# A tile of ones at address 160 instead of 192 modulo 256, in a decoder block bound by TensorE

## The chip, the cores and the metric

The kernel runs on one core of a Trainium2 chip, as one program. The time is the device time of one execution in microseconds. It was run three times before the change: median 1702.03 us, 1701.56 to 1702.17. One more execution was profiled.

## What is computed

One decoder block on 256 tokens of width 2048, all in float32 (heads, masks and gains are left out here):

```python
x = x + hybrid_mixer(rms_norm(x, g_mix), w_in, w_a2, b_a, g_gla, w_pool, pool_scale, w_branch, w_out)
x = x + memory_cross_attention(rms_norm(x, g_cross), rms_norm(mem, g_mem), w_cq, w_ckv, w_co)
x = x + conv_glu_ffn(rms_norm(x, g_ffn), w_up, conv_w, conv_b, w_down)
return rms_norm(x, g_final)

def rms_norm(x, g):
    return x * rsqrt(mean(x * x, axis=-1) + EPS) * g
```

The mixer projects with w_in (2048 x 8208), runs a gated linear attention of four heads and a pooling branch, gates and joins them with w_branch, and projects with w_out. The cross-attention reads 256 memory tokens. The FFN projects up to 2 x 5632 columns, applies a causal convolution of width 3 and a gate, and projects down. Some 77 million weights are each used once for all 256 tokens.

## The kernel before, in words

**Layout.** Activations are kept transposed: features on the 128 partitions, the 256 tokens along the free dimension, 16 chunks of 128 features. A weight matrix comes in units of 2048 x 128 (16 blocks of 128 x 128); each unit yields 128 output features for all tokens.

**Two parts for each number.** To get float32 results from the faster float32r products, each number is split in a high part, rounded to float32r, and a low part, the rest. Weights are split as they arrive: a DMA brings half a unit to a `raw` tile, ScalarE casts the high part to `wh`, VectorE subtracts for the low part `wl` (both at line 110, in `Weights.make`). An activation tile holds, for each chunk, 256 columns high and 256 columns low side by side (`Act`). `products` (lines 316 to 322) runs over the blocks of a unit and issues two matmuls for each, the *pair* that the rest of this text counts: line 321 with the block of `wh` as stationary operand against all 512 columns, line 322 with the block of `wl` against the 256 high columns only. Both add up in one PSUM tile. Stages that use these pairs are, in order: w_in (56 units: keys, queries, r, gates, pool, more gates; tiles ps_k, ps_q, ps_r, ps_g, ps_p), w_branch (br), w_out (ps_wo), the keys of the memory (ps_ck), the queries (ps_cq), the output of the attention (ps_wc), the FFN (88 units ps_up and, in thirds, ps_dn and ps_dl with ps_dt). The values are made the other way round, activations stationary and weights moving, three float32r matmuls each (va at lines 395 to 397, cv at lines 713 to 715).

**Groups in plain float32.** Between the units stand small groups of matmuls on plain float32 operands, which TensorE runs as two passes each (a transpose as one). Their stationary operands are named by `lhsT`. They are: decay gates (L459 a transpose of `a_sb`, L467 with `wa`), scores of the linear attention (L524, L513, L550), its values (L562 to L564), the norm of its heads (L579), the pooling maps (L616), the transposes of the attention weights (L755), and the RMS norms. The norms use the tile `ones`, 128 x 128, in two ways: `Sum.cols` (L270) has the sums of squares as stationary operand and one column of the ones as moving operand; `Sum.rows` (L279) has the ones as stationary operand and a 128 x 256 diagonal, `diag`, moving. L579 has the ones as stationary operand against 512 columns. At the start eight products of the ones with themselves (L348, `warm`) keep TensorE at work until the first weights are there; at the end L892, L893 and L899 use the ones for the last norm. `behind` puts each such group right after a given pair in TensorE's order.

**Order.** One planner orders the instructions of all engines at build time; TensorE's order is otherwise the order of the loops. DMAs of weights are issued from SyncE's queue as the six `raw` tiles come free.

**Addresses.** Tiles of a pool lie one behind the other in each partition, rounded up to 32 bytes; pools lie in the order of their opening, `const` first. The pools `pad1` and `pad2` put 192 and 64 bytes between others. Modulo 256 this gives: `ones` 192, `ident` 192, `a_sb` 32 and 96 (its two halves), all tiles of `big` (activations, kq, kl, v, wa, wp, so and so on) 160, `wh` 96, `wl` 160, `acc` and `diag` 160, the attention weights `pr` 224.

Of the kernel before, what the change touches and what calls it, by code (L numbers as in the profile page):

```python
# [8 lines left out]
F32 = mybir.dt.float32  # L9
# [6 lines left out]
P = 128  # L16
# [126 lines left out]
def block(ctx, tc, xT, memT, vecs, masks, wa2, wpool, w_va, w_in, w_branch, w_out, w_ckv_k, w_ckv_v, w_cq, w_co, w_up, w_down, out):  # L143
    nc = tc.nc
    PS = bass.MemoryType.PSUM
    const = ctx.enter_context(tc.tile_pool(name="const", bufs=1))
# [63 lines left out]
    nc.sync.dma_start(vec[:, V_CB:], vecs[:, V_CB:])  # L210
    eps_t = const.tile([P, 1], F32, name="eps_t")
    nc.vector.memset(eps_t, EPS)
    ones = const.tile([P, P], F32, name="ones")
    ident = const.tile([P, P], F32, name="ident")
    nc.vector.memset(ones, 1.0)
    make_identity(nc, ident)
    scrap = const.tile([P, 1], F32, name="scrap")
# [760 lines left out]
```

## Time and profile before

| | us |
|---|---|
| median of three runs | 1702.03 |
| the profiled execution | 1702.15 |
| its span, first to last instruction | 1700.4 |
| TensorE weight loads busy | 1490.3 |
| VectorE busy | 1228.0 |
| ScalarE busy | 897.2 |
| GpSimd busy | 31.7 |

TensorE's matmuls are PE, its weight loads PEld, VectorE is DVE, ScalarE ACT, GpSimd POOL, SyncE SP. A matmul's duration includes the time in which the next one already runs, so durations add up to more than the time; how fast TensorE goes is read from the starts. `L321` is line 321 of the kernel. The profile's mean DMA rate is 186 GB/s.

### The profile page before, as it was taken

The page shows a single profiled execution, that of the slowest core. Times are in us where ns is not written, and L with a number is a line of the kernel's source. Part 1 is how long each engine was busy: PE and PEld are TensorE (multiplying, and loading weights), DVE is VectorE, ACT ScalarE, POOL GpSimd, SP SyncE. Part 2 cuts the span into 40 slices and gives each one's busy share as a digit, 9 for nine tenths or more (in the row PEclk, how much of TensorE's full clock was granted, in tenths as well). Part 3 has the DMA queues.
Part 4 walks back from the last instruction along what each step waited for, and adds up shares of the span by engine and source line. Part 5 has one row for each costly group of instructions (what it writes and reads, how often), then busy time and mean ns, then how long its engine had stood idle before and what let it go on. Part 6 is the DMA issues. An engine that isn't in the chain of part 4 may idle for free.

```text
span 1700.4 us, 25992 instructions
## 1 busy us (share of the span) xinstructions
PE 1689.0 (99%) x9900; PEld 1490.3 (88%) x9900; DVE 1228.0 (72%) x1904; ACT 897.2 (53%) x1376; POOL 31.7 (2%) x137
## 2 busy tenths in 40 slices
PE   9999999999999999999999999999999999999997
PEld 9988988888888888889988888888888888888887
DVE  7687658667889755447777788775677776567776
ACT  7555456445556544445555655553355554345564
POOL 2000000000001000000000000000000000000000
PEclk9999999999999999999999999999999999999999
DMA  8665556556666566655446665666665566665563
GB/s 276 193 204 166 174 161 208 182 169 196 192 218 218 184 191 188 186 186 167 152 148 191 189 190 190 187 186 187 190 190 188 186 187 188 190 191 186 170 178 112
DMA packets 90734, 316.15 MB, mean 186 GB/s; under 512 B 10208, under 2 KB 11104, under 8 KB 90608
## 3 DMA queue, kind: packets, MB, share of 16 engines
q1 hardware_dynamic: 90464, 314.43, 59.4%
q8 instruction: 77, 1.26, 0.3%
q14 instruction: 49, 0.40, 0.1%
q10 hardware_dynamic: 144, 0.05, 0.0%
HBM read 312.35 MB, written 2.10 MB: 185 GB/s over the span
## 4 chain that ended last, share of the span: by engine, by line
PE 99%; DMA 0%; DVE 0%; SPq 0%; ACT 0%; issue 0%; DVEq 0%; ACTq 0%
PE ps_up L321 19%; PE ps_up L322 10%; PE ps_dn L321 7%; PE ps_g L321 7%; PE ps_dn L322 4%; PE ps_ck L321 3%; PE ps_g L322 3%; PE ps_wc L321 3%; PE ps_wo L321 3%; PE ps_cq L321 3%; PE br L321 3%; PE cv L714 2%; PE ps_ck L322 2%; PE cv L713 2%; PE cv L715 2%; PE ps_p L321 2%
## 5 line engine op out<-in xcount | busy, mean ns | idle before, releaser
L110 DVE TENSOR_TENSOR wl<-raw,wh 128x1024 fp32r<-128x1024 f32 (+3 forms) x602 | 718.1, 1194 | 379.4 <-ACT wh L110 371.9
L110 ACT CAST wh<-raw 128x1024 fp32r<-128x1024 f32 (+3 forms) x602 | 614.6, 1023 | 712.2 <-issue 273.2
L321 PE MATMUL ps_up<-h,wh 128*128 128x512 f32 x1408 | 493.0, 395 | 0.0
L322 PE MATMUL ps_up<-h,wl 128*128 128x256 f32 x1408 | 394.8, 280 | 0.0
L321 PEld LDWEIGHTS ps_up<-h,wh 128*128 128x128 f32 x1408 | 264.7, 188 | 61.1
L322 PEld LDWEIGHTS ps_up<-h,wl 128*128 128x128 f32 x1408 | 264.3, 188 | 0.0
L321 PE MATMUL ps_dn<-ga,wh 128*128 128x512 f32 x512 | 179.3, 395 | 0.0
L321 PE MATMUL ps_g<-h,wh 128*128 128x512 f32 x512 | 178.0, 394 | 0.0
L322 PE MATMUL ps_dn<-ga,wl 128*128 128x256 f32 x512 | 143.6, 280 | 0.0
L322 PE MATMUL ps_g<-h,wl 128*128 128x256 f32 x512 | 142.1, 277 | 0.0
L321 PEld LDWEIGHTS ps_dn<-ga,wh 128*128 128x128 f32 x512 | 96.3, 188 | 22.3
L321 PEld LDWEIGHTS ps_g<-h,wh 128*128 128x128 f32 x512 | 96.2, 188 | 20.7 <-ACT wh L110 0.2
L322 PEld LDWEIGHTS ps_g<-h,wl 128*128 128x128 f32 x512 | 96.2, 188 | 0.3 <-issue 0.2
L322 PEld LDWEIGHTS ps_dn<-ga,wl 128*128 128x128 f32 x512 | 96.1, 188 | 0.0
L321 PE MATMUL ps_ck<-me,wh 128*128 128x512 f32 x256 | 89.7, 395 | 0.0
L321 PE MATMUL ps_cq<-h,wh 128*128 128x512 f32 x256 | 87.8, 390 | 0.0
L321 PE MATMUL ps_wc<-oc,wh 128*128 128x512 f32 x256 | 87.6, 390 | 0.0
L321 PE MATMUL ps_wo<-mg,wh 128*128 128x512 f32 x256 | 87.3, 389 | 0.0
L322 PE MATMUL ps_ck<-me,wl 128*128 128x256 f32 x256 | 71.7, 280 | 0.0
L322 PE MATMUL ps_cq<-h,wl 128*128 128x256 f32 x256 | 70.7, 276 | 0.0
L322 PE MATMUL ps_wc<-oc,wl 128*128 128x256 f32 x256 | 70.5, 276 | 0.0
L322 PE MATMUL ps_wo<-mg,wl 128*128 128x256 f32 x256 | 70.5, 276 | 0.0
(321 smaller groups left out, 2765.5 us busy)
## 6 DMA issues: line engine op xcount, KB each, us to landing
raw<-w_up SPq DMA_DIRECT2D x176, 512.0 KB, 3.6
raw<-w_in SPq DMA_DIRECT2D x112, 512.0 KB, 3.9
raw<-w_down SPq DMA_DIRECT2D x64, 512.0 KB, 3.6
raw<-w_branch SPq DMA_DIRECT2D x32, 512.0 KB, 4.4
raw<-w_out SPq DMA_DIRECT2D x32, 512.0 KB, 4.4
raw<-w_ckv_k SPq DMA_DIRECT2D x32, 512.0 KB, 3.7
raw<-w_ckv_v SPq DMA_DIRECT2D x32, 512.0 KB, 3.5
raw<-w_cq SPq DMA_DIRECT2D x32, 512.0 KB, 4.3
```

Of the source, the lines that this page charges most:

```text
L110: return self.nc.scalar.copy(hi, src), self.nc.vector.tensor_sub(lo, src, hi.bitcast(F32))
L321: nc.tensor.matmul(ps, lhsT=wh, rhs=act.both(c), start=f, stop=False, skip_group_check=True)
L322: pe["last"] = nc.tensor.matmul(ps[:, 0:T], lhsT=wl, rhs=act.hi(c), start=False, stop=l, skip_group_check=True)
L713: nc.tensor.matmul(acc[t], lhsT=xh, rhs=wh, start=c == 0, stop=False)
L714: nc.tensor.matmul(acc[t], lhsT=xh, rhs=wl, start=False, stop=False)
L715: nc.tensor.matmul(acc[t], lhsT=xl, rhs=wh, start=False, stop=c == NC - 1)
```

## The change

Two tiles without any use stand around the ones in the pool `const`: 56 float32 (224 bytes) in front of them, 8 float32 (32 bytes) behind. The ones so begin 224 bytes later, at 160 modulo 256 and no longer at 192; `ident` and all that lies behind it, the other pools too, begins 256 bytes later and keeps its address modulo 256. VectorE sets both new tiles to zero.

```diff
     eps_t = const.tile([P, 1], F32, name="eps_t")
     nc.vector.memset(eps_t, EPS)
+    gaps = [const.tile([P, 56], F32, name="gap0")]
     ones = const.tile([P, P], F32, name="ones")
+    gaps.append(const.tile([P, 8], F32, name="gap1"))
     ident = const.tile([P, P], F32, name="ident")
+    for gap in gaps:
+        nc.vector.memset(gap, 0.0)
     nc.vector.memset(ones, 1.0)
     make_identity(nc, ident)
```

## Rows read from the trace of the kernel before

**Rows 1.** The page: span, TensorE's busy time, the chain that ended last.
```profile
span 1700.4 us, 25992 instructions
...
PE 1689.0 (99%) x9900; PEld 1490.3 (88%) x9900; DVE 1228.0 (72%) x1904; ACT 897.2 (53%) x1376; POOL 31.7 (2%) x137
...
PE 99%; DMA 0%; DVE 0%; SPq 0%; ACT 0%; issue 0%; DVEq 0%; ACTq 0%
```
**Rows 2.** Groups by line, TensorE, 962.5 to 1629.3 us: busy us, mean ns | idle before.
```profile
L321 PE MATMUL ps_up<-h,wh 128*128 128x512 f32 x1376 | 481.9, 395 | 0.0
...
L321 PE MATMUL ps_dn<-ga,wh 128*128 128x512 f32 x512 | 179.3, 395 | 0.0
...
L321 PE MATMUL ps_dl<-ga,wh 128*128 128x512 f32 x18 | 6.3, 395 | 0.0
```
**Rows 3.** Groups by line, TensorE, 325 to 575 us.
```profile
L321 PE MATMUL ps_wo<-mg,wh 128*128 128x512 f32 x256 | 87.3, 389 | 0.0
```
**Rows 4.** Timeline of TensorE from 961.4 us: start us, us, instruction.
```profile
961.82 0.59 PE L279 MATMUL rps_wc<-diag_wc,ones 128*128 128x256 f32 x2
...
962.60 0.40 PE L321 MATMUL ps_up<-h,wh 128*128 128x512 f32 x1
...
966.10 0.40 PE L321 MATMUL ps_up<-h,wh 128*128 128x512 f32 x1
```
**Rows 5.** Timeline of TensorE from 324 us.
```profile
323.83 1.03 PE L616 MATMUL pps<-pl,wp 128*128 128x256 f32 x4
...
325.73 0.39 PE L321 MATMUL ps_p<-h,wh 128*128 128x512 f32 x1
...
328.11 0.39 PE L321 MATMUL ps_p<-h,wh 128*128 128x512 f32 x1
```
**Rows 6.** Timeline of TensorE from 785.9 us.
```profile
786.24 0.60 PE L755 MATMUL pTps<-ident,pr 128*128 128x128 f32 x4
...
787.37 0.39 PE L321 MATMUL ps_cq<-h,wh 128*128 128x512 f32 x1
```
**Rows 7.** Timeline of TensorE from 248.3 us.
```profile
248.45 1.88 PE L579 MATMUL oss<-so,ones 128*128 128x512 f32 x4
...
252.96 0.40 PE L321 MATMUL ps_g<-h,wh 128*128 128x512 f32 x1
```
**Rows 8.** Timeline of TensorE from 61.4 us.
```profile
61.77 0.38 PE L459 MATMUL aps<-ident,a_sb 128*16 128x128 f32 x2
...
63.39 0.40 PE L321 MATMUL ps_k<-h,wh 128*128 128x512 f32 x1
```
**Rows 9.** Timeline of TensorE from 1629 us.
```profile
1629.35 0.74 PE L321 MATMUL ps_dl<-ga,wh 128*128 128x512 f32 x2
...
1631.54 0.39 PE L321 MATMUL ps_dl<-ga,wh 128*128 128x512 f32 x1
```
**Rows 10.** Groups by line, TensorE: 249.8 to 322.8, 582.6 to 660.6, 660.7 to 750.6 us.
```profile
L321 PE MATMUL ps_g<-h,wh 128*128 128x512 f32 x144 | 50.8, 398 | 0.0
...
L321 PE MATMUL ps_p<-h,wh 128*128 128x512 f32 x64 | 22.4, 395 | 0.0
...
L321 PE MATMUL ps_ck<-me,wh 128*128 128x512 f32 x224 | 78.6, 396 | 0.0
...
L714 PE MATMUL cv<-wl,me 128*128 128x512 f32 x128 | 51.0, 399 | 0.0
```
**Rows 11.** Stretches: us, then busy us by engine, clock, DMA share, GB/s.
```profile
370.00:570.00 200.00, 199.99 (x1177) 176.65 (x1176) 167.31 (x258) 115.60 (x194) 11.99 (x14) 1.00 0.64 204
...
970.00:1620.00 650.00, 650.00 (x3716) 569.14 (x3716) 480.73 (x719) 334.32 (x484) 8.43 (x84) 1.00 0.61 187
```
**Rows 12.** Timeline of the start: the memsets, the warm-up, a wait of TensorE.
```profile
0.81 0.12 DVE L159 MEMSET pad<- 128x48 f32 x2 [0.81 <-PEq L971]
...
1.14 3.78 PE L348 MATMUL warm<-ones 128*128 128x128 f32 x16 [1.14 <-DVE ones L215]
...
11.27 0.39 PE L395 MATMUL va<-wh,h 128*128 128x260 f32 x1 [1.10 <-ACT wh L110]
```
**Rows 13.** One stretch, TensorE alone: us, busy us, clock, DMA share, GB/s.
```profile
13.20:16.20 3.00, 3.00 (x16) 0.50 1.05 404
```

## The prediction, made before the changed kernel was run

> **What bounds the kernel now.** I read the page first, from the span to the chain of waits [rows 1]: TensorE is busy for 1689.0 of 1700.4 us, and the chain that ends last runs on it for 99%. So time can only come from work taken off TensorE, or from the same work done there at another rate. The second is the point here, and the groups of instructions by line show it when they are asked stretch by stretch. One unit of weights is 16 pairs (12 in the last down products): L321, the high part of the weights, 512 columns, then L322, the low part, 256 columns. Between 962.5 and 1629.3 us, where TensorE never waits, one L321 has a mean of 395 ns [rows 2]; from 325 to 575 us the same form stands at 389 ns [rows 3]. These durations overlap, so the rate itself is read from starts in the timeline. Behind the group L279 at 961.82 us ten pairs go from 962.60 to 966.10: 350 ns a pair [rows 4]. Behind the group L616 at 323.83 us seven go from 325.73 to 328.11: 340 ns [rows 5]. Same shapes, and TensorE idle in neither. The kernel has **two rates, 340 and 350 ns a pair**, and each lasts for hundreds of pairs; an L321 of 0.40 us in the timeline marks the slow one, 0.39 the fast one.
>
> What sets the rate? Each slow stretch begins right behind a small group of products in plain float32, and I compared those groups by the tile that they hold as stationary operand. There are 28 places where such a group is followed by pairs. Behind 24 of them the pairs fall to 340 ns after two or three: L467, L524, L513, L550, L562 to L564 and L616, whose stationary tiles lie at 160 modulo 256 (one row group stands for these, [rows 5]); L270, stationary the sums of squares, also at 160, and the ones only moving, one column; L755, stationary at 224 [rows 6]. Behind the other four the pairs stay at 350 ns: L579 at 248.45 [rows 7], the two L279 in the keys and the one at 961.82 [rows 4], which are all the groups with the ones, at 192, as stationary operand that are followed by pairs; and L459 at 61.77, with a stationary operand of 16 columns, slow for 14 pairs until L467 [rows 8]. Length doesn't sort them: the group L755 takes 0.60 us and L279 0.59. Nor does the moving operand: L755 streams ident, at 192, and the pairs behind it are fast. What sorts 27 of the 28 is whether the stationary operand begins at 160 or 224 (32 above a multiple of 64) or at 192 (on one). Once set, a rate stays until something breaks the order of TensorE: the next float32 group, the products L713 to L715, or the odd place at 1629.35 where two L321 stand side by side, behind which the pairs are fast [rows 9].
>
> **The change part by part.**
>
> *The ones at 160.* L279 with the ones there has the addresses modulo 256 and the form of L616: stationary 128x128 at 160, moving 128x256 at 160. L616 is followed by fast pairs 4 times of 4. So I take it that the three stretches behind L579 and L279 go at 340 ns. Their pairs: 1376 + 512 + 18 = 1906 in the FFN [rows 2], 224 in the keys, 144 + 64 = 208 in gates and pool [rows 10], 2338 together. Two or three pairs are slow behind fast groups too, so 3 x 3 come off: 2329 x 10 ns = 23.3 us. The other 1864 or so (4216 by the loops, less 2338, less 14) are fast already. Bounds: nothing, if the address isn't the cause; and above, L714 behind the slow keys stands at 399 ns [rows 10], and if it and its neighbours, 384 in all, fell to the 389 of [rows 3], 3.8 us more. I take nothing for them: their operands keep their places, and the pairs behind them are fast now.
>
> *What the faster pairs ask of the others.* In the FFN 350 to 340 asks 2.9% more of the other engines. From 970 to 1620 us VectorE is busy for 480.73 of 650 us, 74%, ScalarE for 51%, and DMA moves 187 GB/s. From 370 to 570 us, at 340 ns a pair, VectorE is at 167.31 of 200, 84%, DMA at 204 GB/s, and TensorE is busy for all but 0.01 us [rows 11]. The FFN at 340 ns would need 76% and 192 GB/s, both below what is carried there. So nothing is late next, and the sum holds in full.
>
> *The products with the ones themselves.* Two of L279 take 0.59 us and four of L616, at 160, take 1.03 [rows 4, 5]: 0.22 for each one more, the same 0.37 for the last. I take no change. Behind the warm-up, all of them are some 8 us; 3%, the only difference of rates seen here, is 0.3 us either way.
>
> *The two memsets.* VectorE sets two tiles of 48 elements in 0.12 us, so 56 and 8 elements cost some 0.06 each. They may stand ahead of the ones, for which the warm-up L348 waits, so the first product may come up to 0.12 us later. TensorE then waits 1.10 us for a cast at 11.27 [rows 12], which a DMA feeds, and that takes the delay up: nothing; without that cover 0.12. What a shifted start can touch is the clock: from 13.2 to 16.2 us, behind such waits, the granted clock is 0.50, the lower of its two levels, and 16 products take 3.0 us [rows 13] that go at 0.12 each at full clock. Having that stretch or not is worth 1.1 us either way; I take none, as the runs of before lie within 0.6.
>
> *Two rules weighed.* The Trainium skill, "TensorE: Matmul & The Clock Gate", step-by-step of a matmul, says that TensorE has two independent read ports and that "loading the next tile's weights doesn't steal SBUF read bandwidth from the running matmul"; and the Trainium skill, "SBUF — State Buffer", specifications, gives lines of 16 bytes, on which 160 and 192 both begin. By these no address of the ones could change a rate, and the time would be that of rival (d). The trace agrees in part only: two rates with the same shapes and no wait [rows 2, 3] show that something beyond two free streams costs 10 ns a pair; that it is the address, no run here has shown.
>
> **Sum.** The profiled execution took 1702.15 us, 1700.4 of it the span; 1702.15 - 23.3 = 1678.8. The median shown, 1702.03, lies 0.12 below that execution, which gives **1678.7 us**.
>
> **The rivals.** (a) is the forecast: all three stretches turn fast, 1678.7. For it: 27 of 28 groups, and that fast is what the other disturbances fall to. (b) The FFN turns fast, the keys or the gates don't: 2.2 and 2.1 us are missing, 1680.8 to 1683.0. For it: L579 streams 512 columns, a form that none of the fast groups has. (c) Only keys or gates turn: 1697.7 to 1699.9. For it: the group at 961.82 is one lone product of two passes, and the fast groups of this width have eight. (d) Nothing turns, 1702.0: the rate is set by something else that goes with these groups, such as so few passes of 256 or more columns, or the same stationary tile loaded again each time. All three groups share that, so the trace can't tell it from the address. Against it: neither explains L459, nor do few passes alone, since L755 has four. (e) Slower: everything behind the tile lies 256 bytes further. If a longer period than 256 decides which rate pairs fall to, fast stretches turn slow at 10 ns a pair: with w_out and the query and output products of the attention, 768 pairs, 7.7 us more, 1709.7; with all 1864, 18.6 us, 1720.6. It decides from some 340 pairs on. Against it: the places of all other tiles to each other stay, and the fast rate outlives every border between units now.
>
> **How the numbers follow.** (a) 0.56, (b) 0.12, (c) 0.07, (d) 0.17, (e) 0.08. A measurement of this kernel tells some 0.2%, 3.4 us, from no change. Faster: (a), (b) and half of (c), 0.72; same: (d) and the other half, 0.20; slower: 0.08. The likeliest case has its own range, 1674.5 (L713 to L715 in its favour, with the 0.3 of the ones' own products) to 1681. Ended there the range would leave more than three in ten out, and at 1700 still a quarter, so it goes to 1702.6, no change with the memsets' 0.12 and the spread of the runs: 1674.5 to 1702.6.
>
> **What would show it.** Right: behind L279, then near 959 us, successive L321 start 0.34 us apart, L321 has a mean of 389 ns in ps_up and ps_dn, in ps_ck, and in the ps_g and ps_p behind L579, and the 14 pairs behind L459 stay slow. Wrong: 395 ns in ps_up as before (then the address is not it); a stretch that is fast now at 395 (e); or TensorE waiting for wl or wh in the FFN, where the cover would be too thin.

## The result, and the profile after

The kernel with the ones at 160 takes **1679.13 us** (median of four executions, 1678.34 to 1680.02); in the same runs the kernel before took 1702.10 (1701.56 to 1702.72). The ratio is 0.9865, 95% interval 0.9848 to 0.9882. The forecast was 1678.7.

The page of the profiled execution, 1678.34 us, answers to [rows 1]: the span is 23.9 us shorter, TensorE's busy time 24.4, and the chain still runs on TensorE for 98%. The amount of work is the same.

```profile
span 1676.5 us, 25994 instructions
...
PE 1664.6 (99%) x9900; PEld 1475.7 (88%) x9900; DVE 1228.2 (73%) x1906; ACT 898.8 (54%) x1376; POOL 31.9 (2%) x137
...
PE 98%; DVE 0%; ACT 0%; DMA 0%; SPq 0%; issue 0%; DVEq 0%; ACTq 0%
```

Below the new lines everything in the kernel after stands 4 lines further down: L325 and L326 are the pair that stood at L321 and L322. Groups by line, TensorE, 957.5 to 1609.5 us (busy us, mean ns | idle before). They answer to [rows 2]: 395 has become 389; for ps_dn the same view gives 389 too.

```profile
L325 PE MATMUL ps_up<-h,wh 128*128 128x512 f32 x1376 | 468.2, 389 | 0.0
```

Timeline of TensorE behind the group of the FFN, as in [rows 4] (start us, us, instruction). From 958.06 to 960.10 are six pairs: 340 ns each, where the kernel before had 350.

```profile
956.93 0.59 PE L283 MATMUL rps_wc<-diag_wc,ones 128*128 128x256 f32 x2
...
958.06 0.39 PE L325 MATMUL ps_up<-h,wh 128*128 128x512 f32 x1
...
960.10 0.39 PE L325 MATMUL ps_up<-h,wh 128*128 128x512 f32 x1
```

The same view behind the group of the gates, as in [rows 7]: six pairs from 250.24 to 252.28, 340 ns again. The four products of the group take 1.88 us, as before.

```profile
247.83 1.88 PE L583 MATMUL oss<-so,ones 128*128 128x512 f32 x4
...
250.24 0.39 PE L325 MATMUL ps_g<-h,wh 128*128 128x512 f32 x1
...
252.28 0.39 PE L325 MATMUL ps_g<-h,wh 128*128 128x512 f32 x1
```

Behind the transpose of `a_sb`, which the change leaves alone, the pairs are as slow as in [rows 8].

```profile
61.15 0.38 PE L463 MATMUL aps<-ident,a_sb 128*16 128x128 f32 x2
...
62.07 0.40 PE L325 MATMUL ps_k<-h,wh 128*128 128x512 f32 x1
...
62.42 0.40 PE L325 MATMUL ps_k<-h,wh 128*128 128x512 f32 x1
```

Groups by line, TensorE, of the stretches of [rows 10]: gates and pool 249.4 to 322, keys 579.5 to 656.5, values 655.5 to 746 us. The keys fall from 396 to 390; the middle product of the values stays at 399.

```profile
L325 PE MATMUL ps_g<-h,wh 128*128 128x512 f32 x144 | 49.4, 392 | 0.0
...
L325 PE MATMUL ps_ck<-me,wh 128*128 128x512 f32 x224 | 76.4, 390 | 0.0
...
L718 PE MATMUL cv<-wl,me 128*128 128x512 f32 x128 | 51.0, 399 | 0.0
```

The FFN as one stretch (us; busy us of PE, PEld, DVE, ACT, POOL; clock, DMA share, GB/s), against the second line of [rows 11]: VectorE at 483.19 of 635 us is 76%, DMA at 192 GB/s, TensorE never waits.

```profile
965.00:1600.00 635.00, 635.00 (x3738) 562.25 (x3737) 483.19 (x723) 338.29 (x489) 8.33 (x84) 1.00 0.62 192
```

Counted start by start over both traces, 2413 pairs of the kernel before took about 350 ns (345 to 355) and 86 of the kernel after do: 2327 x 10 ns = 23.3 us. The other 0.6 us of the two profiled executions lie at the start, where the first pair of all begins at 55.69 in place of 56.31 us (rows of the timeline, then the stretch as above). VectorE's memsets delay the first product from 1.14 to 1.22 us, but TensorE's wait of 1.10 us in [rows 12] is now 0.55, and from 13.2 to 16.2 us the granted clock is 1.00, the upper of the two levels, where [rows 13] had 0.50.

```profile
1.22 3.15 PE L352 MATMUL warm<-ones 128*128 128x128 f32 x13 [1.22 <-DVE ones L219]
...
10.86 0.39 PE L399 MATMUL va<-wh,h 128*128 128x260 f32 x1 [0.55 <-ACT wh L110]
```

```profile
13.20:16.20 3.00, 3.00 (x28) 3.00 (x26) 3.00 (x5) 3.00 (x9) 1.81 (x2) 1.00 1.05 405
```

### The profile page after: what moved, and what is told of

It is laid out like the page before. It is cut to its first block, busy times and chain, and to the rows that moved or that the text cites. A ratio compares the mean times of both kernels' runs of the same rounds, so it can differ in the third digit from the quotient of the medians.

```text
span 1676.5 us, 25994 instructions
## 1 busy us (share of the span) xinstructions
PE 1664.6 (99%) x9900; PEld 1475.7 (88%) x9900; DVE 1228.2 (73%) x1906; ACT 898.8 (54%) x1376; POOL 31.9 (2%) x137
## 4 chain that ended last, share of the span: by engine, by line
PE 98%; DVE 0%; ACT 0%; DMA 0%; SPq 0%; issue 0%; DVEq 0%; ACTq 0%
PE ps_up L325 19%; PE ps_up L326 10%; PE ps_g L325 7%; PE ps_dn L325 7%; PE ps_wc L325 3%; PE ps_dn L326 3%; PE ps_g L326 3%; PE ps_wo L325 3%; PE br L325 3%; PE ps_ck L325 3%; PE ps_cq L325 3%; PE cv L718 2%; PE cv L717 2%; PE cv L719 2%; PE ps_cq L326 2%; PE ps_ck L326 2%
## 5 line engine op out<-in xcount | busy, mean ns | idle before, releaser
L325 PE MATMUL ps_up<-h,wh 128*128 128x512 f32 x1408 | 479.3, 389 | 0.0
L326 PE MATMUL ps_up<-h,wl 128*128 128x256 f32 x1408 | 388.6, 276 | 0.0
L325 PEld LDWEIGHTS ps_up<-h,wh 128*128 128x128 f32 x1408 | 264.3, 188 | 54.9
L326 PEld LDWEIGHTS ps_up<-h,wl 128*128 128x128 f32 x1408 | 264.3, 188 | 0.0
L325 PE MATMUL ps_g<-h,wh 128*128 128x512 f32 x512 | 176.6, 392 | 0.0
L325 PE MATMUL ps_dn<-ga,wh 128*128 128x512 f32 x512 | 174.2, 389 | 0.0
L326 PE MATMUL ps_g<-h,wl 128*128 128x256 f32 x512 | 141.4, 276 | 0.0
L326 PE MATMUL ps_dn<-ga,wl 128*128 128x256 f32 x512 | 141.3, 276 | 0.0
L325 PEld LDWEIGHTS ps_g<-h,wh 128*128 128x128 f32 x512 | 96.2, 188 | 20.0 <-ACT wh L110 0.2
L325 PEld LDWEIGHTS ps_dn<-ga,wh 128*128 128x128 f32 x512 | 96.1, 188 | 19.9
L326 PEld LDWEIGHTS ps_g<-h,wl 128*128 128x128 f32 x512 | 96.2, 188 | 0.3 <-issue 0.2
L326 PEld LDWEIGHTS ps_dn<-ga,wl 128*128 128x128 f32 x512 | 96.1, 188 | 0.0
L325 PE MATMUL ps_cq<-h,wh 128*128 128x512 f32 x256 | 87.8, 390 | 0.0
L325 PE MATMUL ps_wc<-oc,wh 128*128 128x512 f32 x256 | 87.6, 390 | 0.0
L325 PE MATMUL ps_ck<-me,wh 128*128 128x512 f32 x256 | 87.5, 390 | 0.0
L325 PE MATMUL ps_wo<-mg,wh 128*128 128x512 f32 x256 | 87.3, 389 | 0.0
L326 PE MATMUL ps_cq<-h,wl 128*128 128x256 f32 x256 | 70.7, 276 | 0.0
L326 PE MATMUL ps_ck<-me,wl 128*128 128x256 f32 x256 | 70.7, 276 | 0.0
L326 PE MATMUL ps_wc<-oc,wl 128*128 128x256 f32 x256 | 70.5, 276 | 0.0
L326 PE MATMUL ps_wo<-mg,wl 128*128 128x256 f32 x256 | 70.5, 276 | 0.0
```

Source lines behind the costliest of these rows:

```text
L325: nc.tensor.matmul(ps, lhsT=wh, rhs=act.both(c), start=f, stop=False, skip_group_check=True)
L326: pe["last"] = nc.tensor.matmul(ps[:, 0:T], lhsT=wl, rhs=act.hi(c), start=False, stop=l, skip_group_check=True)
```

## Experiments

A time that stands without a range is that of one execution, the profiled one.

### Only the shift of all else by 256 bytes

```diff
-    gaps = [const.tile([P, 56], F32, name="gap0")]
+    gaps = []
     ones = const.tile([P, P], F32, name="ones")
-    gaps.append(const.tile([P, 8], F32, name="gap1"))
+    gaps.append(const.tile([P, 64], F32, name="gap1"))
```

> The ones back at 192, with one gap of 256 bytes behind them, so that everything else lies as in the changed kernel and the two memsets less one are there too. Theory (the address of the ones as stationary operand sets the rate of the pairs behind): gates and pool behind L579, keys and FFN go at 350 ns a pair again, 2327 pairs x 10 ns = 23.3 us over 1679.1, so 1702.4. Rival (the shift of everything else by 256 bytes, or the changed start, made the pairs fast): they stay at 340 ns, 1679.1.

Measured: 1702.1 (1701.34 to 1702.96), ratio to the kernel before 1.0, interval 0.9991 to 1.001; the same 2413 pairs are slow. TensorE's groups by line from 965 to 1605 us show the old mean:

```profile
L325 PE MATMUL ps_up<-h,wh 128*128 128x512 f32 x1317 | 461.1, 395 | 0.0
```

So neither the other tiles' new places nor the memset change the rates (this kernel has one memset more than the kernel before, the changed kernel two). Rival (e) falls, and with it the thought that the start made the difference. What acts is where the ones themselves lie.

### Other addresses for the ones

Each of the three groups gets a tile of ones of its own, at an address chosen through the gap ahead of it (here 128 for the gates, 32 for the keys, 64 for the FFN; the other three kernels have other gaps, the third and fourth of the table slices of wider tiles too). The first kernel of the table also has `a_sb` 32 bytes further, at 64 and 128.

```diff
-    gaps.append(const.tile([P, 8], F32, name="gap1"))
+    for i, (key, skip, wide, at) in enumerate([('o', 56, 128, 0), ('mem', 40, 128, 0), ('wc', 8, 128, 0)]):
...
+        more.append(const.tile([P, wide], F32, name=f"ones_{key}"))
+        some[key] = more[-1][:, at : at + P]
...
-            nc.tensor.matmul(ps, lhsT=ones, rhs=diag, start=True, stop=True)
+            nc.tensor.matmul(ps, lhsT=some.get(self.name, ones), rhs=diag, start=True, stop=True)
```

> As the changed kernel, but three more tiles of ones: at 224 for L579, at 0 for the two L279 in the keys, at 96 for the L279 in the FFN; a_sb moved by 32 bytes to 64 and 128. Theory (32 above a multiple of 64 is fast, on a multiple slow): gates and pool 340 ns, keys 350, FFN 340, so 1679.1 + 2.2 = 1681.3. Rival (only 160, the place of the moving operand, is fast): all three slow, 1702.4. The 14 pairs behind L459 have no forecast: at 96 its 16 columns were slow, so if its rule is the other way round they turn fast (0.14 us, seen in the trace alone).

> As the last, with the ones at 128 for L579, at 32 for the keys, at 64 for the FFN, a_sb in its old place. Theory (by 64): gates and pool 350 ns, keys 340, FFN 350, so 1679.1 + 2.1 + 19.0 = 1700.2. Rival (only 160 is fast): all slow, 1702.4. Rival (only 192 is slow): all fast, 1679.1.

> How fine the rule is: the ones at 176 for L579, at 144 for the keys, at 168 for the FFN, as slices of wider tiles. If the upper half of each 64 bytes is fast: gates and pool 340 ns, keys 350, FFN 340, 1681.3. If only the multiple of 64 itself is slow: all 340, 1679.1. If only 32 above a multiple is fast: all 350, 1702.4.

> The changed kernel with three tiles of ones, at 64 for the gates (L579), 200 for the keys, 184 for the FFN. Theory A (slow only where the operand begins at 64 modulo 128 exactly): gates slow, keys and FFN fast: 1679.1 + 205 x 10 ns = 1681.2. Theory B (slow in the whole block of 32 bytes from 64 modulo 128): gates and keys slow, 1683.4. Rival C (64 was slow in the FFN for its own reasons and the gates don't care): 1679.1 or, with the keys alone, 1681.3.

Measured, with the rate of nearly all pairs behind each group:

| gates | keys | FFN | us |
|---|---|---|---|
| 224: 340 | 0: 340 | 96: 340 | 1679.51 |
| 128: 340 | 32: 340 | 64: 350 | 1697.89 |
| 176: 340 | 144: 340 | 168: 340 | 1678.95 |
| 64: 340 | 200: 340 | 184: 350 | 1698.04 |

A row of each of the two kernels with a slow FFN, timeline of TensorE: first 64, then 184. Behind both, the pairs start 0.35 us apart.

```profile
958.32 0.40 PE L334 MATMUL ps_up<-h,wh 128*128 128x512 f32 x1
...
958.67 0.40 PE L334 MATMUL ps_up<-h,wh 128*128 128x512 f32 x1
```

```profile
958.32 0.40 PE L333 MATMUL ps_up<-h,wh 128*128 128x512 f32 x1
...
958.66 0.40 PE L333 MATMUL ps_up<-h,wh 128*128 128x512 f32 x1
```

The address of the ones matters, but the rule of the prediction doesn't hold: 0 and 128 are multiples of 64 and fast. After three of these kernels "64 modulo 128 is slow" fitted all; the fourth ended that too: 64 is fast in front of the gates, and 184 slow in front of the FFN. In the first kernel the 14 pairs behind the transpose of `a_sb` stay at 350 ns, so its two new addresses, 64 and 128, change nothing.

### One more product behind the group

A plain float32 product of one column right behind `rps_wc`: in the kernel before, with a fast operand (at 160); in the kernel after, with a slow one (`ident`, at 192).

```diff
+        nc.tensor.matmul(ps[:, 0:1], lhsT=s_f.acc[:, 0:P], rhs=ones[:, 0:1], start=True, stop=True)
```

```diff
+        nc.tensor.matmul(ps[:, 0:1], lhsT=ident, rhs=ones[:, 0:1], start=True, stop=True)
```

> The kernel before, the ones still at 192, with one plain float32 product of one column added right behind rps_wc, 16 pairs into the FFN: stationary the squares' sum at 160, moving a column of the ones at 192; its result is copied to a scrap tile. Theory (the stationary operand of the last plain float32 group decides the rate): the FFN's 1906 pairs behind it go at 340 ns, 19 us less than 1702.1, plus some 0.5 for the product itself: 1683.6, keys and gates still slow. Rival (what decides is the group rps_wc as a whole, its two passes of 256 columns or the ones as such, and one column can't undo it): 1702.6.

> The changed kernel, the ones at 160, with one plain float32 product of one column added right behind rps_wc: stationary the identity, which lies at 192, moving a column of the ones at 160. Theory (the stationary operand of the last group decides, at 64 modulo 128 the slow way): the FFN falls back to 350 ns a pair, 1906 x 10 ns = 19.1 us more than 1679.1 and 0.5 for the product: 1698.7. Rival (any short product resets the pairs to the fast rate, or only the ones make them slow): 1679.6.

Measured: 1685.78 and 1697.99. Timelines of TensorE, the first kernel and then the second: 340 ns a pair behind the one (965.17 to 966.87 are five pairs), 350 behind the other, for nearly all 1906 pairs in both.

```profile
964.60 0.28 PE L832 MATMUL touch<-ones,acc_wc 128*128 128x1 f32 x2
...
965.17 0.39 PE L321 MATMUL ps_up<-h,wh 128*128 128x512 f32 x1
...
966.87 0.39 PE L321 MATMUL ps_up<-h,wh 128*128 128x512 f32 x1
```

```profile
957.74 0.28 PE L836 MATMUL touch<-ones,ident 128*128 128x1 f32 x2
...
958.31 0.40 PE L325 MATMUL ps_up<-h,wh 128*128 128x512 f32 x1
...
958.66 0.40 PE L325 MATMUL ps_up<-h,wh 128*128 128x512 f32 x1
```

One column is enough to change the rate of 1906 pairs, so the ones' group has no lasting hold on TensorE: what comes after it can undo it. That the last product decides by itself isn't shown; the test bed below speaks against it. The first kernel missed its forecast by 2.2 us, and that is the more telling part. Groups by line of w_out, 490 to 574 us in the kernel before, then 489 to 577 in this one:

```profile
L321 PE MATMUL ps_wo<-mg,wh 128*128 128x512 f32 x235 | 79.9, 389 | 0.0
```

```profile
L321 PE MATMUL ps_wo<-mg,wh 128*128 128x512 f32 x237 | 83.0, 395 | 0.0
```

Here both programs have the same instructions at the same addresses; the added product comes some 477 us later. At 487.10 two L321 stand side by side in this trace, and behind them 254 pairs are slow: 2.5 us. The kernel after has the same odd place at 484.71 and stays fast. So no address has to move for the rate to change; where TensorE's order is disturbed, the pairs can fall to either side.

### The diagonal at 192

```diff
-            diag = sm.tile([P, T], F32, tag="sq", name=f"diag_{self.name}", bufs=3)
+            if self.name in some:
+                diag = big.tile([P, 1024], F32, tag="u", name=f"diag_{self.name}")[:, 8 : 8 + T]
```

> The changed kernel with the diagonal, the moving operand of L279, at 192 and no longer at 160; the ones at 224 for the keys and at 192 for the FFN, at 160 for the gates. Theory A (the stationary operand's own address decides, slow at 64 modulo 128): keys and gates fast, FFN slow: 1679.1 + 19.1 = 1698.2. Theory B (its distance to the moving operand decides, slow where it is 32 more modulo 128): keys slow, FFN fast: 1681.3.

Measured: 1699.04; keys and gates at 340 ns, the FFN at 350. With the moving operand 32 bytes on, 192 is slow in the FFN as before, and 224 is fast in the keys, so the distance between the two operands isn't the rule (one place each).

### Many groups in one kernel

```diff
+        nc.tensor.matmul(ps[:, 0:n], lhsT=probe[:, at : at + P], rhs=s_f.acc[:, 0:n], start=True, stop=True)
...
+            behind(touch, *tries[2 * j + g])
...
+            if swap == i:
+                b()
+                pe["last"] = a()
```

> The changed kernel as a test bed, its time of no interest. Behind each of the 88 units of ps_up stands one more plain float32 product, stationary a slice of a tile of ones that begins at 0, 32, 64, ... 224 modulo 256, moving the squares' sum (at 160), one column or 256 of it; the 16 cells of address and width come in shuffled order, 5 or 6 times each. In the down products, one unit in two ends with such a product at 160 of 1 to 192 columns, and in the others L322 is issued ahead of L321 once, at the ninth pair. What counts is the rate of the pairs behind each. Theory A (the address decides, 64 and 192 slow): all stretches behind 22 of the 88 at 350 ns, those behind the other 66 at 340 ns, whatever the width, and all 16 of 160 fast. Theory B (the address and the form together): the cells differ, each cell the same in its repeats. Theory C (the pairs fall into one of two rhythms by the nanosecond at which they start, and address and width only shift that): the same cell gives both rates in its repeats, or the widths at 160 alternate. Where an odd order decides, it brings both rates. Time: 44 x 0.23 + 44 x 0.55 + 16 x 0.3 = 39 us for the products, and 10 ns for each slow pair, 3.5 us by A: about 1722.

Measured: 1718.74. Of the 88 stretches in ps_up, 56 end at 340 and 32 at 350 ns. Behind each cell, in the order of its repeats (F: 340, S: 350, from the starts in the trace):

```
address   1 column       256 columns
0         F F F F F S    F F F S F
32        F F F S F S    S S S S S S
64        F F F F F      S S S S S S
96        F S S S S F    F F F F F
128       F F F F F      F F F F F F
160       F F F F F      F F F F F
192       F F F F F      S S S S S
224       S S S S S F    F S S F F F
```

Two of the timelines, TensorE, 256 columns each, operand at 160 and at 192: 340 ns and 350 ns a pair.

```profile
957.96 0.59 PE L845 MATMUL touch<-acc_wc,probe 128*128 128x256 f32 x2
...
959.09 0.39 PE L327 MATMUL ps_up<-h,wh 128*128 128x512 f32 x1
...
959.43 0.39 PE L327 MATMUL ps_up<-h,wh 128*128 128x512 f32 x1
```

```profile
969.52 0.59 PE L845 MATMUL touch<-acc_wc,probe 128*128 128x256 f32 x2
...
970.65 0.40 PE L327 MATMUL ps_up<-h,wh 128*128 128x512 f32 x1
...
971.00 0.40 PE L327 MATMUL ps_up<-h,wh 128*128 128x512 f32 x1
```

Ten of the 16 cells are the same in every repeat, so it isn't chance; but the width counts as much as the address (192 is slow with 256 columns and fast with one), so theory A falls. The mixed cells are not random either. Most of them follow the rate that the pairs had *before* the group: at 32 with one column the result was each time the other rate than before (6 of 6), at 96 with one column too (6 of 6), at 224 with 256 columns and at 0 with one each time the same (6 of 6 twice). Cell and rate before together leave 2 of 87 cases open; with 29 such combinations that describes these cases and was tested on no others. That lies between theories B and C. A reading that fits, but that nothing here shows directly, is that the group shifts the pairs by an amount that its operands and width set, so that where they land depends on where they were.

The cells don't carry over to other places either. At 32 with 256 columns all six are slow here, and the keys behind the ones at 32 (two such products, one behind the other) were fast; at 192 with one column all five are fast here, and the product with `ident`, also at 192 and of one column, but right behind `rps_wc`, was followed by slow pairs. So more than the address and width of the last product counts.

In the down products, theory A had all 16 products at 160 fast; behind 15 of them the pairs were at 340 ns, behind the one of 16 columns, which found them at 350, they stayed there. All 16 units in which L322 once goes first end at 340 ns, but 15 were there already; only the one behind the 16 columns came from 350.

### The odd order alone

In the kernel before, with the ones at 192, the third pair behind each of the three groups is turned round.

```diff
-        products(ps, terms(W.get(unit), act, n))
+        products(ps, terms(W.get(unit), act, n), swap=2 if name in ("g7_1", "ck2", "up1_0") else None)
...
+            for matmul in (low, high) if i == swap else (high, low):
```

> The kernel before, the ones at 192, with nothing moved: at three places, in the first unit behind L579, behind L279 of the keys and behind L279 of the FFN, the third pair is issued L322 first and L321 second. Theory (the pairs are in one of two rhythms, the group with the ones leaves them in the slow one, and an odd order puts them in the fast one, as it did 16 times of 16 in the down products): 4 or 5 pairs are slow at each of the three places, the other 2330 or so turn to 340 ns, the odd order itself costs some 0.03 us: 1702.1 - 23.2 = 1678.9. Rival (the address of the ones keeps the rate down as long as they were the last plain float32 operand): 1702.1.

Measured: 1681.29 (1679.66 to 1683.41); the kernel before had 1704.09 (1702.18 to 1707.2) in these runs; ratio 0.9869, interval 0.985 to 0.9888, as large a gain as that of the change. Timeline of TensorE: behind the turned pair (two L322, then two L321) the starts are 0.34 apart, 961.63 to 962.99 for four pairs, with the same ones at 192.

```profile
959.81 0.59 PE L279 MATMUL rps_wc<-diag_wc,ones 128*128 128x256 f32 x2
...
960.82 0.40 PE L322 MATMUL ps_up<-h,wl 128*128 128x256 f32 x2
961.06 0.62 PE L321 MATMUL ps_up<-h,wh 128*128 128x512 f32 x2
...
961.63 0.39 PE L321 MATMUL ps_up<-h,wh 128*128 128x512 f32 x1
...
962.99 0.39 PE L321 MATMUL ps_up<-h,wh 128*128 128x512 f32 x1
```

This decides against any rule by which the address of the ones keeps the rate down: it only chose the start. The kernel before ran 2.0 us longer in these runs than in those of the result; no trace shows why. In the profiled execution, 1681.21 us, the excess over the forecast is w_out again, 254 slow pairs or 2.5 us:

```profile
L321 PE MATMUL ps_wo<-mg,wh 128*128 128x512 f32 x228 | 79.8, 395 | 0.0
```

### The operands of the pairs themselves

The halves of a unit's weights begin at other places, unit by unit; first in steps of 32 bytes over all 256, then in steps of 4 to 8 around the place of now. The pools `pad1` and `pad2` are left out, as the places are set by the slices.

```diff
+        a, b = self.at.get(i, (SHIFT, 0))
...
-                hi = self.his.tile([P, half], F32R, tag="wh", name=f"wh{i}_{h}", padded_shape=[P, UNIT])
-            lo = self.los.tile([P, half], F32R, tag="wl", name=f"wl{i}_{h}", padded_shape=[P, UNIT])
+                hi = self.his.tile([P, UNIT + 64], F32R, tag="wh", name=f"wh{i}_{h}")[:, a : a + half]
+            lo = self.los.tile([P, UNIT + 64], F32R, tag="wl", name=f"wl{i}_{h}")[:, b : b + half]
```

> The changed kernel, with the weight tiles of the FFN's ps_up and first two ps_dn moved unit by unit: wh at 160, 192, ... 128 and wl at 160, 192, ... 128 modulo 256, all 64 pairs of places once or twice in shuffled order; before the FFN both as in the changed kernel, behind it wh at 96 and wl at 160. Theory A (the pairs know two rhythms, 340 and 350 ns, wherever their operands lie; a place can at most tip them from one into the other): every unit at 340 or 350, between 1679 and 1698 us. Theory B (the places of wh and wl set the rate, and some pair of places is better than that of now): some units below 340 ns, at best 320, the 768 columns at 2.4 GHz, the same in both their repeats. Theory C (places can be worse): some units above 350 ns and the kernel over 1700 us.

> As in the run with all pairs of places, but in fine steps around the place of now: wh at 96 and wl at 160 modulo 256, each by -24, -16, -8, 0, 8, 16 or 24 bytes, all 49 combinations twice in two different orders, then some of 4 and 12 bytes, the last two units at the place of now. Theory A (what counts is the block of 32 bytes in which an operand begins): the 16 combinations with both at 0 to 24 bytes go at 340 ns and those with a negative step at 346 to 354. Theory B (the exact byte counts): only 96 and 160 themselves, or few places, at 340, or a new rate below 340 somewhere, at best 320. In the first case some 40 of the 120 units keep 340 ns and 80 lose 10 ns a pair: 1679.1 + 80 x 16 x 0.010 = 1692; in the second nearer to 1701.

Measured: 1701.09 and 1694.87. In the first, TensorE was busy for all of the stretch from 961 to 1610 us at full clock:

```profile
961.00:1610.00 649.00, 649.00 (x3715) 568.51 (x3714) 481.74 (x720) 337.59 (x487) 8.40 (x84) 1.00 0.63 187
```

and yet a unit's mean time per pair ran from 340 to 353 ns. Timelines of TensorE, a unit with wh at 96 and wl at 160, then one with both at 192; fifteen pairs each, 340 and 353 ns:

```profile
1380.54 0.39 PE L325 MATMUL ps_up<-h,wh 128*128 128x512 f32 x1
...
1385.64 0.39 PE L325 MATMUL ps_up<-h,wh 128*128 128x512 f32 x1
...
1391.43 0.40 PE L325 MATMUL ps_up<-h,wh 128*128 128x512 f32 x1
1391.79 0.39 PE L325 MATMUL ps_up<-h,wh 128*128 128x512 f32 x1
1392.13 0.40 PE L325 MATMUL ps_up<-h,wh 128*128 128x512 f32 x1
...
1396.73 0.39 PE L325 MATMUL ps_up<-h,wh 128*128 128x512 f32 x1
```

In the second unit the starts are 0.36 and 0.34 apart by turns: a rhythm of its own. Of 64 places two kept 340 ns, wh at 96 or 224 with wl at 160; the others went at 346 to 353, most in rhythms of two or three pairs (347, 346, 347 or 353, 354, 353), and of the 56 places that came twice, 55 gave the same mean within 1 ns. But those came in the same order twice, so 55 of the 56 also had the same place just ahead of them. The fine steps, in two different orders: wh at 96 with wl at 160 gave 340 six times of six, a few neighbours too (72 with 160 or 176; 96 with 172; 108 with 160), but wh at 100 gave 347, at 104 347 and 353, and 108 with 172 even 367. Timelines, wh at 100 and then at 96, wl at 160: four starts, 1.04 us for three pairs, against 1.02.

```profile
1494.71 0.39 PE L325 MATMUL ps_up<-h,wh 128*128 128x512 f32 x1
...
1495.75 0.39 PE L325 MATMUL ps_up<-h,wh 128*128 128x512 f32 x1
...
1604.99 0.39 PE L325 MATMUL ps_up<-h,wh 128*128 128x512 f32 x1
...
1606.01 0.39 PE L325 MATMUL ps_up<-h,wh 128*128 128x512 f32 x1
```

Of the 52 places that came more than once here, nine went at two rates more than 2 ns apart (last nine pairs of a unit), six of these within one and the same stage. Timelines, wh at 96 and wl at 144 both times: nine pairs take 3.12 us the first time, 3.18 the second, 347 and 353 ns.

```profile
1070.46 0.39 PE L325 MATMUL ps_up<-h,wh 128*128 128x512 f32 x1
...
1073.58 0.39 PE L325 MATMUL ps_up<-h,wh 128*128 128x512 f32 x1
...
1277.27 0.40 PE L325 MATMUL ps_up<-h,wh 128*128 128x512 f32 x1
...
1280.45 0.40 PE L325 MATMUL ps_up<-h,wh 128*128 128x512 f32 x1
```

So theory A of both kernels falls. Theory C of the first holds: 353 ns, and 1701.09 us. Theory B holds in part: the place of the operands, by single words, changes the rate, but at some places more than one rate is possible; there the operands and places are the same, and what ran before is not. That this is what chooses wasn't tested by itself. The hope in it doesn't hold: none of the 127 places of both kernels went below 340 ns, so none of those tried is better than that of now.

## Why the prediction was right, and where it was not

**Two rates, and all three stretches turn.** Right: behind L583 and the L283 of the keys and of the FFN nearly all pairs go at 340 ns. The prediction's 2329 pairs at 10 ns were 2327, so the sum of 23.3 us came out.

**The cause.** The step "the stationary operand's address of the last plain float32 group decides, 32 above a multiple of 64 fast, on a multiple slow" was right for 160 and 192 and wrong as a rule. Ones at 0, 128 and, for the gates, 64 are fast; at 184 the FFN is slow. What the runs show in its place: at the place where this kernel's weights lie, the pairs have two rhythms that sustain themselves, 340 and 350 ns. A group or an odd order can move them from one to the other; which one they fall into depends on the address, the width and the rhythm before, and on more than these. The 27 of 28 groups that spoke for the rule looked like 27 witnesses but held three addresses: 160 in 20 of them, 224 in four, 192 in three. They showed that 160 is good here (25 of 26 products in the test bed, the one of 16 columns aside) and little more. That was enough for the number, since the change went to 160 and L616, at the same addresses as the new L283, was fast 4 times of 4; that it held for L579, with 512 columns, was in part luck, and by the same rule the ones at 0 would have been forecast slow, which in the keys they weren't. Nor is fast what all disturbances fall to, as rival (a) had it: behind the odd place in w_out the pairs were slow in three of the 14 traces.

**Nothing late next.** Right to the figure: 76% and 192 GB/s were expected, and measured.

**L713 to L715.** Taken as no gain, and there was none: the 399 ns of L714 are the 399 of L718. The bound of 3.8 us below wasn't used.

**The memsets and the start.** The first product comes 0.08 us later, hidden as argued. The slow clock of [rows 13] went away in the profiled execution, where the start gains the 0.6 us beyond the sum; the prediction had bounded that at 1.1 us either way and taken none. It isn't shown to come from the change: that stretch has 1.00 with the ones back at 192 too, and 0.52, nearly the lower level, in the kernel with the diagonal at 192. That the medians, 22.97 us apart, contain it isn't shown either.

**The rivals.** (d) and (e) are refuted by the result, (e) by the first experiment too; (b) and (c) didn't occur, but the kernel with the ones at 64, 200 and 184 is of kind (c), at 1698.04, so they were no idle bounds. Rival (d) had a true part: one short product or one turned pair makes the pairs fast without any other address for the ones.

**The two rules.** Both kernels that move the pairs' own operands bear on them. With the same instructions, no wait of TensorE and a granted clock of 1.00, the rate runs from 340 to 367 ns by where the weights begin. By the Trainium skill, "TensorE: Matmul & The Clock Gate", Step-by-step: what each phase is for, loading doesn't take read bandwidth from the running matmul; that may be so of bandwidth, but the time of a load and matmul pair is not free of the addresses here. Nor does the line of 16 bytes of the Trainium skill, "SBUF — State Buffer", Specifications (TRN2), settle it: 96 and 104 lie in one such line, and wh went at 340 ns at the one and at 347 or 353 at the other.

**Open.** What in the chip makes the rhythms isn't known, and no rule found here tells ahead which address or order gives the fast one. Whether the moving operand's address shifts the start as the stationary one's does was tried at one place only. Why the transpose of `a_sb` leaves 14 slow pairs isn't known; moving it by 32 bytes, tried once, didn't change it. And the odd place in w_out may cost the kernel after 2.5 us in an execution, as it did in three other kernels' profiles here; its own four times, within 1.7 us, don't show it.

## What to carry to other kernels

Where one engine is busy for the whole span, read the starts of its repeated instructions, not only its busy share: two rates for the same shapes, each lasting for hundreds of instructions, mean that time may be had without touching the work, here 1.35%. Look for what stands at the changes between them, and try both a shift of the operands and one exchange in the order, since either tipped the rhythm here. And count the distinct values among the witnesses of a rule, not the witnesses: here a rule on addresses rested on three of them.

## What the runs showed of the hardware

- A chain of load and matmul pairs on TensorE held a rate for some 1900 pairs after one event: 340 or 350 ns, with no wait of TensorE. Within a pair, the step from the 512-column to the 256-column matmul is 227 or 233 ns, and the step back 113 or 117.
- A product of one column, behind which the next pair began 0.14 us later, changed the rate of the 1906 pairs behind it, 19 us in sum, once each way.
- The rate depends on where the stationary operands begin, by single words of 4 bytes: 340 ns with wh at 96, 347 at 100 (wl at 160); 367 was the slowest, and 340 the fastest of 127 places. At nine of 52 places it was another when the place came again.
- One pair turned round, L322 first, was followed by 340 ns a pair in 19 places of 19, four of which were at 350 before it. The odd order in w_out, two L321 and then two L322, went to either side: 340 in 11 traces, 350 in three.
